# Last product of a down projection by quarters of the tokens: a hybrid encoder layer on one core

## The chip, the cores and the metric

The kernel runs on one NeuronCore of one Trainium2 chip. The metric is the device time of one execution in microseconds (us), median of the runs shown. Six names of engines occur: PE is TensorE's matrix multiplication, PEld its weight load, DVE is VectorE, ACT is ScalarE, POOL is GpSimd, and SP is SyncE, which here only issues DMA transfers. A letter q behind an engine (SPq, ACTq) means its queue of instructions.

## The reference, cut to what matters

One layer on 1024 tokens of width 1024: a normalised input, two attention mixers, an output projection with residual, then a gated MLP with residual, and a final RMS norm. The change lies in the last two lines:

```python
def rmsnorm(x, g):
    xf = x.astype(jnp.float32)
    y = xf * lax.rsqrt(jnp.mean(xf * xf, axis=-1, keepdims=True) + EPS)
    return (y * g.astype(jnp.float32)).astype(x.dtype)

def conv_gated_mlp(h, w_gate, w_up, conv_w, conv_b, w_down):
    ...
    return jnp.einsum('bsf,fd->bsd', jax.nn.silu(g) * u, w_down)

    h = h + conv_gated_mlp(hn, w_gate[l], w_up[l], conv_w[l], conv_b[l], w_down[l])
    return rmsnorm(h, norm_final)
```

The hidden width of the MLP is 2816, that is 22 tiles of 128, and `w_down` takes it back to 1024, that is 8 tiles of 128.

## The kernel before

Everything is held transposed: the 128 partitions carry 128 of the 1024 features, and the tokens run along the free dimension. `res[d]` (d from 0 to 7) is the residual stream of feature tile d, 128 partitions by 1024 tokens; the program's names in the profile show it as `h`. The tokens fall into two halves of 512 (`HALF`), h = 0 and h = 1, and `tsl(h)` is the slice of half h.

**Arithmetic.** Each fp32 operand is split into two fp32r parts, high and low, and a product of 128 hidden features takes three matmuls of 128 by 512: high by high, high by low, low by high. That is `group` (lines 797 to 799); every one of the three loads its own weights. Plain fp32 matmuls with a small moving operand (the sums `ss` and the spreadings `sw` below) show as two passes each in the trace.

**The down projection by seven products.** The product of w_down with the activations is cut into 2 by 2 blocks (features in lower and upper four tiles, hidden width in two halves of 11 tiles, tokens in two halves) and done as seven block products, `PRODUCTS`, p = 0 to 6. Within a product j runs over 0 to 3; a pair is the feature tiles j and j + 4. c runs over the three parts of the 11 hidden tiles (`PARTS`: 4, 4 and 3). `order` lists all (p, j, c), and from p = 1 on j is the outer of the two inner loops. Each step of the loop (line 1227 on) calls `prepare(i + 6, i + 4)`, which starts the loads of weights six steps ahead and splits the weights four steps ahead; then `group` for the step; then at most one task of `todo`. When a (p, j) is finished, `leave` is put in `todo`: DVE adds the PSUM bank to `res` (line 1188), and where that tile is then final, ACT squares it (line 1192) and DVE adds the square to a running sum (line 1197). Product 6 finishes tiles 4 to 7 of half 0; tiles 0 to 3 of half 0 and all tiles of half 1 are final before it. In the last `leave` (tile 7, half 0) the last square is not added; `inverse_narrow` takes both summands.

**The final norm.** `inverse_narrow` (line 145) sums the squares over the 128 partitions by matmuls with a column of ones, a token tile c of 128 at a time, into `ss`, column c; ACT takes the square root (line 153) and DVE the reciprocal (line 154). The result has the tokens on the partitions. `widen` (line 157) spreads it: a matmul per token tile of a broadcast column by the identity writes the factor of each token to all 128 partitions, into PSUM bank `sw` (line 161). [...] The tiles `y`, `wide`, `s2` and others share one tag (`tt`) with six buffers.

**The order of the end.** PE's order is the one written in the program (`manual_schedule` for PE); the other engines' orders are made by a scheduler from the program's order and its own estimates. Within product 6: after (j, c) = (0, 2) the `inverse_narrow` of half 1; after (1, 2) its `finish`; then pairs 2 and 3; and behind the last matmul, with nothing left for PE, the last `leave`, `inverse_narrow` and `finish` of half 0.

Of the kernel before, what the change touches and what calls it, by code (L numbers as in the profile page):

```python
# [15 lines left out]
AF = mybir.ActivationFunctionType  # L16
ALU = mybir.AluOpType
# [3 lines left out]
KT = D // 128  # L21
# [30 lines left out]
def hybrid_layer(tc, xT, w_in, w_out, w_gate, w_up, w_down, small, sink, rpb, consts, rope, out):  # L52
    nc = tc.nc
    with ExitStack() as ctx:
# [87 lines left out]
                acc = s2  # L142
            return acc

        def inverse_narrow(sqs, dim, tag):

            ps = bank("ss", tag)
            for c in range(4):
                for i, sq in enumerate(sqs):
                    nc.tensor.matmul(ps[:, c:c + 1], sq[:, c * 128:(c + 1) * 128], ones[:, 0:1], start=c == 0 and i == 0,  # L150
                                     stop=i == len(sqs) - 1, skip_group_check=True)
            v = cpool.tile([128, 4], F32, name="v4", tag="v4", bufs=4)
            nc.scalar.activation(v, ps[:, 0:4], AF.Sqrt, bias=eps, scale=float(D) / dim)
            nc.vector.reciprocal(v, v)
            return v

        def widen(v, tag):

            wide = bank("sw", tag)
            for c in range(4):  # L160
                nc.tensor.matmul(wide[:, c * 128:(c + 1) * 128], v[:, c:c + 1].to_broadcast([128, 128]), ident, start=True, stop=True)
            return wide

        def inverse_rms_wide(sq, dim, tag):
# [630 lines left out]
        def group(ps, ws, xs, first, last):  # L795
            for i, (w, x) in enumerate(zip(ws, xs, strict=True)):
                nc.tensor.matmul(ps, w[0], x[0], start=first and i == 0, stop=False, skip_group_check=True)  # L797
                nc.tensor.matmul(ps, w[0], x[1], start=False, stop=False, skip_group_check=True)  # L798
                nc.tensor.matmul(ps, w[1], x[0], start=False, stop=last and i == len(ws) - 1, skip_group_check=True)  # L799
# [384 lines left out]
            x_split(0, k)  # L1184
        sq, todo, vs = {}, [], {}

        def add(d, h, ps):
            nc.vector.tensor_tensor(res[d][:, tsl(h)], ps, res[d][:, tsl(h)], op=ALU.add)

        def square(d, h):  # L1190
            s2 = half("s2")
            nc.scalar.activation(s2, res[d][:, tsl(h)], AF.Square)
            if (d, h) == (KT - 1, 0):
                sq[h] = [sq[h], s2]
                return
            if h in sq:
                nc.vector.tensor_tensor(s2, s2, sq[h], op=ALU.add)
            sq[h] = s2

        def finish(h, v, tag):  # L1200
            wide = widen(v, tag)
            copy = half("wide")
            nc.scalar.activation(copy, wide, AF.Copy)
            for d in range(KT):
                y = half("y")
                x = res[d][:, tsl(h)]
                if d % 3 == 2:
                    nc.scalar.activation(y, x, AF.Copy, scale=col(C_NFIN + d))  # L1208
                    nc.gpsimd.tensor_tensor(y, y, copy, op=ALU.mult)  # L1209
                else:  # L1210
                    nc.vector.scalar_tensor_tensor(y, x, col(C_NFIN + d), wide, op0=ALU.mult, op1=ALU.mult)
                nc.sync.dma_start(out[d, :, tsl(h)], y)

        def leave(p, j, ps):

# [3 lines left out]
            else:  # L1219
                d, h = {1: (lo, 0), 2: (hi, 1), 3: (lo, 1), 4: (lo, 1), 5: (hi, 1), 6: (hi, 0)}[p]  # L1220
                add(d, h, ps)
                if p in (1, 4, 5, 6):
                    square(d, h)

        tags = lambda j, y: ("s", "s", "pt", "pt")[j] if y else ("pj", "pj", "o", "o")[j]
        banks = {}
        for i, (p, j, c) in enumerate(order):
            prepare(i + 6, i + 4)
            f, n = PARTS[c]
            if p in (0, 2, 3) and c == 0:  # L1230
                banks[p, j] = bank("dn", tags(j, p == 2))
            else:
                banks[p, j] = banks[{0: 0, 1: 0, 2: 2, 3: 3, 4: 2, 5: 3, 6: 3}[p], j]
            ps = banks[p, j]
            at_start, at_end = c == 0 and p in (0, 2, 3), c == 2
            group(ps, dws.pop((p, j, c)), [xs[p, f + q] for q in range(n)], at_start, at_end)
            if todo:
                todo.pop(0)()
            if at_end:
# [111 lines left out]
```

## Time and profile before

| | |
|---|---|
| median of 3 runs | 1128.92 us (1128.06 to 1130.89) |
| profiled execution | 1127.34 us |
| its span | 1125.6 us |
| granted TensorE clock, mean | 0.984 |

All times of rows below are from the start of that span. A row of the timeline gives the start, the duration, engine and line, the operation, output and inputs by name, the tile's shape, how many instructions the row merges, and in brackets how long the engine had been idle and what released it. A row of the windows view gives, for a stretch A:B, its length, then the busy time (and number of instructions) of PE, PEld, DVE, ACT and POOL, then the granted clock as a share of full speed, the busy share of the 16 DMA engines, and the GB/s moved. A matmul's duration holds its way through the pipeline; its cost in a stream is the distance to the next start.

### The profile page before, as it was taken

How to read it: one execution, taken by the hardware profiler on the slowest of the kernel's cores; microseconds unless marked ns; L12 is line 12 of the kernel's file. 1: busy time of each engine (PE TensorE's matmuls, PEld its weight loads, DVE VectorE, ACT ScalarE, POOL GpSimd, SP SyncE). 2: the span in 40 equal slices, each digit the busy share in tenths (PEclk: the TensorE clock that was granted, in tenths of full speed). 3: DMA queues.
4: the chain of work that ended last, by engine and by line, in shares of the span. 5: the costliest groups of instructions: out<-in, count | busy, mean ns of one | idle time of the engine just before them, and what ended most of it. 6: DMA issues, size and time to landing. Idle time of an engine off the chain costs nothing.

```text
span 1125.6 us, 14912 instructions
## 1 busy us (share of the span) xinstructions
PE 1086.2 (96%) x5124; PEld 903.0 (80%) x5124; DVE 852.4 (76%) x1549; ACT 548.3 (49%) x1033; POOL 105.7 (9%) x186
## 2 busy tenths in 40 slices
PE   8969999999999999999999999999999999999995
PEld 6858888888878877888788888888888878888884
DVE  6557888766689666989988778877877868797843
ACT  7235767655667433445434334334343645543531
POOL 0212332233223100000000000000000000000001
PEclk8989999999999999999999999999999999999997
DMA  7253220333215316412443223222322799875823
GB/s 266 65 122 80 53 57 29 84 92 87 75 31 148 103 47 211 163 47 78 166 160 122 105 92 123 102 103 94 122 103 94 244 302 294 268 221 174 272 83 144
DMA packets 67708, 147.03 MB, mean 131 GB/s; under 512 B 8112, under 2 KB 16816, under 8 KB 67632
## 3 DMA queue, kind: packets, MB, share of 16 engines
q1 hardware_dynamic: 57552, 121.04, 34.6%
q10 hardware_dynamic: 10080, 25.04, 5.9%
q8 instruction: 40, 0.66, 0.2%
q14 instruction: 36, 0.29, 0.1%
HBM read 103.58 MB, written 28.57 MB: 117 GB/s over the span
## 4 chain that ended last, share of the span: by engine, by line
PE 86%; DVE 7%; DMA 3%; ACT 2%; issue 2%; SPq 0%; POOLq 0%; ACTq 0%; DVEq 0%
PE pj L113 7%; PE pj L114 7%; PE pj L115 7%; PE dn L797 6%; PE dn L799 6%; PE dn L798 6%; PE z L799 5%; PE z L797 5%; PE z L798 5%; PE x L797 3%; PE x L799 3%; PE x L798 3%; PE s L273 3%; PE y L799 3%; PE y L797 3%; PE y L798 3%
## 5 line engine op out<-in xcount | busy, mean ns | idle before, releaser
L797 PE MATMUL dn<-xd,whi 128*128 128x512 f32 x308 | 120.2, 390 | 1.1 <-ACT c L1218 1.1
L786 ACT ACTIVATE whi<-ws 128x512 fp32r<-128x512 f32 (+1 forms) x100 | 60.1, 622 | 123.9 <-DVE ws L903 76.3
L799 PE MATMUL dn<-xd,wlo 128*128 128x512 f32 x308 | 119.8, 389 | 0.0
L798 PE MATMUL dn<-xd,whi 128*128 128x512 f32 x308 | 119.8, 389 | 0.0
L799 PE MATMUL z<-hg,wlo 128*128 128x512 f32 x264 | 103.1, 390 | 0.7 <-DVE wlo L787 0.7
L113 PE MATMUL pj<-xgh,whi 128*128 128x512 f32 x248 | 103.4, 417 | 0.0
L797 PE MATMUL z<-hg,whi 128*128 128x512 f32 x264 | 102.9, 390 | 0.0
L798 PE MATMUL z<-hg,whi 128*128 128x512 f32 x264 | 102.7, 389 | 0.0
L299 ACT ACTIVATE p<-p,nm 128x385 f32<-128x385 f32 (+3 forms) x128 | 75.1, 586 | 56.3 <-DVE nm L295 52.3
L115 PE MATMUL pj<-xgh,wlo 128*128 128x512 f32 x248 | 97.7, 394 | 0.0
L114 PE MATMUL pj<-xgl,whi 128*128 128x512 f32 x248 | 97.5, 393 | 0.0
L303 POOL TENSOR_SCALAR p<-p,sm 128x384 f32<-128x384 f32 (+1 forms) x128 | 73.5, 588 | 237.3 <-DVE sm L301 218.2
L787 DVE TENSOR_TENSOR wlo<-raw,whi 128x512 fp32r<-128x512 f32 (+1 forms) x102 | 66.3, 669 | 22.7 <-ACT whi L786 22.5
L787 DVE TENSOR_TENSOR wlo<-ws,whi 128x512 fp32r<-128x512 f32 (+1 forms) x100 | 66.7, 681 | 19.5 <-ACT whi L786 19.5
L309 DVE TENSOR_TENSOR pl<-pt,ph 128x384 fp32r<-128x384 f32 (+2 forms) x108 | 63.1, 588 | 23.2 <-ACT ph L308 22.1
L786 ACT ACTIVATE whi<-raw 128x512 fp32r<-128x512 f32 (+1 forms) x102 | 60.4, 611 | 41.4 <-DMA raw<-in_w_down_dram 18.4
L1108 ACT ACTIVATE xd<-xd 128x512 fp32r<-128x512 f32 x77 | 47.3, 627 | 58.0 <-DMA xd<-x 56.5
L308 ACT ACTIVATE ph<-pt 128x384 fp32r<-128x384 f32 (+2 forms) x108 | 55.3, 514 | 38.2 <-PE pt L408 30.8
L1209 POOL TENSOR_TENSOR y<-y,wide 128x512 f32<-128x512 f32 x4 | 5.1, 1283 | 727.0 <-ACT y L1208 727.0
L799 PE MATMUL y<-hg,wlo 128*128 128x512 f32 x176 | 68.7, 390 | 0.5 <-DVE wlo L787 0.5
L797 PE MATMUL x<-hg,whi 128*128 128x512 f32 x176 | 68.7, 390 | 0.0
L799 PE MATMUL x<-hg,wlo 128*128 128x512 f32 x176 | 68.5, 389 | 0.0
(199 smaller groups left out, 2657.8 us busy)
## 6 DMA issues: line engine op xcount, KB each, us to landing
xd<-x SPq DMA_DIRECT2D x77, 256.0 KB, 5.1
raw<-in_w_down_dram SPq DMA_DIRECT2D x72, 256.0 KB, 3.4
raw<-in_w_gate_dram SPq DMA_DIRECT2D x22, 512.0 KB, 3.5
raw<-in_w_up_dram SPq DMA_DIRECT2D x22, 512.0 KB, 4.0
x<-c ACTq DMA_DIRECT2D x22, 512.0 KB
raw<-in_w_in_dram SPq DMA_DIRECT2D x32, 256.0 KB, 3.2
raw<-in_w_down_dram SPq DMA_DIRECT2D x36, 192.0 KB, 3.8
x<-t ACTq DMA_DIRECT2D x11, 512.0 KB, 2.6
```

What stands on the lines that cost most here:

```text
L113: nc.tensor.matmul(ps, w[0], x[0][:, tsl(h)], start=first, stop=False)
L114: nc.tensor.matmul(ps, w[0], x[1][:, tsl(h)], start=False, stop=False)
L115: nc.tensor.matmul(ps, w[1], x[0][:, tsl(h)], start=False, stop=last)
L299: nc.scalar.activation(p[:, j, 0:e], p[:, j, 0:e], AF.Exp, bias=nm, scale=-1.0, accum_out=sm[:, j:j + 1])
L303: nc.gpsimd.tensor_scalar(p[:, i, 0:m], p[:, i, 0:m], sm[:, i:i + 1], 1.0, op0=ALU.mult, op1=ALU.mult)
L308: nc.scalar.activation(ph[:, 0:n], ps[:, 0:n], AF.Copy)
L309: nc.vector.tensor_tensor(pl[:, 0:n], ps[:, 0:n], f32(ph[:, 0:n]), op=ALU.subtract)
L786: nc.scalar.activation(hi, src, AF.Copy)
L787: nc.vector.tensor_tensor(lo, src, f32(hi[:, :, :]), op=ALU.subtract)
L797: nc.tensor.matmul(ps, w[0], x[0], start=first and i == 0, stop=False, skip_group_check=True)
L798: nc.tensor.matmul(ps, w[0], x[1], start=False, stop=False, skip_group_check=True)
L799: nc.tensor.matmul(ps, w[1], x[0], start=False, stop=last and i == len(ws) - 1, skip_group_check=True)
```

## The change

In product 6, pairs 2 and 3 are no longer done by 512 tokens but by 256: first both pairs for the first quarter of the tokens, then both for the second (the weights of both pairs are kept for that). Half 0's norm, outputs and stores are done for each quarter by itself: those of the first quarter between the matmuls of the second, those of the second behind the last matmul. `leave_quarter` adds and squares 256 columns. `widen` is called twice, into two banks, one read by DVE and one by ACT for the copy. Outputs overwrite `res` instead of going to `y`. The scaling of tiles 2 and 5 by the gain (`scaled`) is a call of its own, placed earlier, and these two tiles come last in `finish`. The second quarter's stores go alternately to SP's and ACT's queue. In `inverse_narrow` the loop over summands is now the outer one, everywhere.

```diff
-        def inverse_narrow(sqs, dim, tag):
+        def inverse_narrow(sqs, dim, tag, n=4):
 
             ps = bank("ss", tag)
-            for c in range(4):
-                for i, sq in enumerate(sqs):
+            for i, sq in enumerate(sqs):
+                for c in range(n):
                     nc.tensor.matmul(ps[:, c:c + 1], sq[:, c * 128:(c + 1) * 128], ones[:, 0:1], start=c == 0 and i == 0,
                                      stop=i == len(sqs) - 1, skip_group_check=True)
...
-        def widen(v, tag):
+        def widen(v, tag, n=4):
 
             wide = bank("sw", tag)
-            for c in range(4):
-                nc.tensor.matmul(wide[:, c * 128:(c + 1) * 128], v[:, c:c + 1].to_broadcast([128, 128]), ident, start=True, stop=True)
+            for c in range(n):
+                nc.tensor.matmul(wide[:, c * 128:(c + 1) * 128], v[:, c:c + 1].to_broadcast([128, 128]), ident,
+                                 start=c == 0, stop=True, skip_group_check=True)
...
-            if (d, h) == (KT - 1, 0):
-                sq[h] = [sq[h], s2]
-                return
...
-        def finish(h, v, tag):
-            wide = widen(v, tag)
+        APART = (2, 5)
+
+        def scaled(d, h):
+            x = res[d][:, tsl(h)]
+            nc.scalar.activation(x, x, AF.Copy, scale=col(C_NFIN + d))
+
+        def finish(h, v, cols=whole, split=False):
+            n = (cols.stop - cols.start) // 128
+            wide, again = widen(v, "pt", n), widen(v, "pt", n)
             copy = half("wide")
-            nc.scalar.activation(copy, wide, AF.Copy)
-            for d in range(KT):
-                y = half("y")
-                x = res[d][:, tsl(h)]
-                if d % 3 == 2:
-                    nc.scalar.activation(y, x, AF.Copy, scale=col(C_NFIN + d))
-                    nc.gpsimd.tensor_tensor(y, y, copy, op=ALU.mult)
+            nc.scalar.activation(copy[:, cols], again[:, 0:128 * n], AF.Copy)
+            for i, d in enumerate([d for d in range(KT) if d not in APART] + list(APART)):
+                x = at_res(d, h, cols)
+                if d in APART:
+                    nc.gpsimd.tensor_tensor(x, x, copy[:, cols], op=ALU.mult)
                 else:
-                    nc.vector.scalar_tensor_tensor(y, x, col(C_NFIN + d), wide, op0=ALU.mult, op1=ALU.mult)
-                nc.sync.dma_start(out[d, :, tsl(h)], y)
+                    nc.vector.scalar_tensor_tensor(x, x, col(C_NFIN + d), wide[:, 0:128 * n], op0=ALU.mult, op1=ALU.mult)
+                (nc.scalar if split and i % 2 else nc.sync).dma_start(out[d, :, h * HALF + cols.start:h * HALF + cols.stop], x)
...
+        def leave_quarter(j, ps, cols):
+
+            x = at_res(j + NP, 0, cols)
+            add(j + NP, 0, ps, cols)
+            s2 = parts[cols.start, j] = half("s2")[:, cols]
+            nc.scalar.activation(s2, x, AF.Square)
+            if j + NP < KT - 1:
+                nc.vector.tensor_tensor(s2, s2, sq[0][:, cols], op=ALU.add)
...
-            group(ps, dws.pop((p, j, c)), [xs[p, f + q] for q in range(n)], at_start, at_end)
+            if p < 6 or j < 2:
+                group(ps, dws.pop((p, j, c)), [xs[p, f + q] for q in range(n)], at_start, at_end)
...
             if p == 6 and (j, c) == (0, 2):
+                for d in APART:
+                    scaled(d, 1)
                 vs[1] = inverse_narrow([sq[1]], D, "s")
             if p == 6 and (j, c) == (1, 2):
-                finish(1, vs[1], "pt")
-        for t in todo:
-            t()
-        finish(0, inverse_narrow(sq[0], D, "s"), "pt")
+                finish(1, vs[1])
+
+
+        parts = {}
+        for k, cols in enumerate(quarters):
+            for j in (2, 3):
+                ps = banks[6, j]
+                for c, (f, n) in enumerate(PARTS):
+                    group(ps[:, cols], dws[6, j, c], [[y[:, cols] for y in xs[6, f + q]] for q in range(n)], False, c == 2)
+                    if todo:
+                        todo.pop(0)()
+                    if (k, j, c) == (0, 3, 0):
+                        for d in APART:
+                            scaled(d, 0)
+                    if (k, j, c) == (1, 2, 0):
+                        vs[0] = inverse_narrow([parts[0, 2], parts[0, 3]], D, "s", 2)
+                    if (k, j, c) == (1, 2, 1):
+                        finish(0, vs[0], quarters[0])
+                leave_quarter(j, ps, cols)
+        first = quarters[1].start
+        finish(0, inverse_narrow([parts[first, 2], parts[first, 3]], D, "s", 2), quarters[1], True)
```

Two things of the changed program's order of instructions are not in the diff. The scheduler moves three of the four `scaled` operations further forward on ACT, to just behind the squares of their tiles (tile 2 of half 0 as far as product 1); the one of tile 5, half 0, stands behind its last square in product 6. And in the last `finish` it puts POOL's stores forward: SP issues those of tiles 0, 2, 3, 6 in this order, ACT those of tiles 1, 5, 4, 7, though tiles 2 and 5 are POOL's and come last in the program. The stores of the first quarter keep the program's order on SP.

More of the change, by code (lines that the diff above doesn't have):

```diff
@@ L152, in inverse_narrow @@
             v = cpool.tile([128, 4], F32, name="v4", tag="v4", bufs=4)
-            nc.scalar.activation(v, ps[:, 0:4], AF.Sqrt, bias=eps, scale=float(D) / dim)
-            nc.vector.reciprocal(v, v)
+            nc.scalar.activation(v[:, 0:n], ps[:, 0:n], AF.Sqrt, bias=eps, scale=float(D) / dim)
+            nc.vector.reciprocal(v[:, 0:n], v[:, 0:n])
             return v
-        def widen(v, tag):
+        def widen(v, tag, n=4):
             wide = bank("sw", tag)
-            for c in range(4):
-                nc.tensor.matmul(wide[:, c * 128:(c + 1) * 128], v[:, c:c + 1].to_broadcast([128, 128]), ident, start=True, stop=True)
+            for c in range(n):
+                nc.tensor.matmul(wide[:, c * 128:(c + 1) * 128], v[:, c:c + 1].to_broadcast([128, 128]), ident,
+                                 start=c == 0, stop=True, skip_group_check=True)
             return wide
@@ L1185, in hybrid_layer, with add @@
         sq, todo, vs = {}, [], {}
-        def add(d, h, ps):
-            nc.vector.tensor_tensor(res[d][:, tsl(h)], ps, res[d][:, tsl(h)], op=ALU.add)
+        whole, quarters = slice(0, HALF), (slice(0, HALF // 2), slice(HALF // 2, HALF))
+        at_res = lambda d, h, cols: res[d][:, h * HALF + cols.start:h * HALF + cols.stop]
+        def add(d, h, ps, cols=whole):
+            x = at_res(d, h, cols)
+            nc.vector.tensor_tensor(x, ps[:, cols], x, op=ALU.add)
         def square(d, h):
@@ L1198, in square @@
             sq[h] = s2
[L1200 to L1212 removed]
+        APART = (2, 5)
[5 more added lines that the diff above has]
+            wide, again = widen(v, "pt", n), widen(v, "pt", n)
+            copy = half("wide")
+            nc.scalar.activation(copy[:, cols], again[:, 0:128 * n], AF.Copy)
+            for i, d in enumerate([d for d in range(KT) if d not in APART] + list(APART)):
+                x = at_res(d, h, cols)
+                if d in APART:
+                    nc.gpsimd.tensor_tensor(x, x, copy[:, cols], op=ALU.mult)
+                else:
+                    nc.vector.scalar_tensor_tensor(x, x, col(C_NFIN + d), wide[:, 0:128 * n], op0=ALU.mult, op1=ALU.mult)
+                (nc.scalar if split and i % 2 else nc.sync).dma_start(out[d, :, h * HALF + cols.start:h * HALF + cols.stop], x)
         def leave(p, j, ps):
@@ L1235, in hybrid_layer @@
             at_start, at_end = c == 0 and p in (0, 2, 3), c == 2
-            group(ps, dws.pop((p, j, c)), [xs[p, f + q] for q in range(n)], at_start, at_end)
+            if p < 6 or j < 2:
+                group(ps, dws.pop((p, j, c)), [xs[p, f + q] for q in range(n)], at_start, at_end)
             if todo:
                 todo.pop(0)()
-            if at_end:
+            if at_end and (p < 6 or j < 2):
                 todo.append(lambda p=p, j=j, ps=ps: leave(p, j, ps))
```

## The prediction

> **What bounds the kernel now.** I read the page first, then the timeline of the last 33 us, then the same end by windows.
>
> ```profile
> span 1125.6 us, 14912 instructions
> ...
> PE 1086.2 (96%) x5124; PEld 903.0 (80%) x5124; DVE 852.4 (76%) x1549; ACT 548.3 (49%) x1033; POOL 105.7 (9%) x186
> ...
> PE 86%; DVE 7%; DMA 3%; ACT 2%; issue 2%; SPq 0%; POOLq 0%; ACTq 0%; DVEq 0%
> ```
>
> PE sets the time nearly everywhere, so more work put among its matmuls is paid in full. The exception is the end:
>
> ```profile
> 1093.68 1.05 PE L161 MATMUL sw<-cst,v 128*128 128x128 f32 x8
> ...
> 1094.49 0.48 PE L797 MATMUL dn<-xd,whi 128*128 128x512 f32 x1
> ...
> 1094.81 0.39 PE L798 MATMUL dn<-xd,whi 128*128 128x512 f32 x1
> ...
> 1109.34 0.39 PE L799 MATMUL dn<-xd,wlo 128*128 128x512 f32 x1
> ...
> 1109.77 0.69 DVE L1188 TENSOR_TENSOR h<-dn,h 128x512 f32<-128x512 f32 x1 [5.29 <-PE dn L799]
> 1110.50 0.63 ACT L1192 ACTIVATE s<-h 128x512 f32<-128x512 f32 x1 [6.74 <-DVE h L1188]
> 1111.18 1.72 PE L150 MATMUL ss<-ones,s 128*128 128x1 f32 x14 [1.33 <-ACT s L1192]
> 1112.94 0.26 ACT L153 ACTIVATE v<-ss,eps 128x4 f32<-128x4 f32 x1 [1.81 <-PE ss L150]
> 1113.23 0.18 DVE L154 RECIPROCAL v<-v 128x4 f32<-128x4 f32 x1 [2.77 <-ACT v L153]
> 1113.47 2.08 PE L161 MATMUL sw<-cst,v 128*128 128x128 f32 x8 [0.57 <-DVE v L154]
> 1115.63 0.60 ACT L1203 ACTIVATE wide<-sw 128x512 f32<-128x512 f32 x1 [2.43 <-PE sw L161]
> ...
> 1116.26 2.72 DVE L1211 SCALAR_TENSOR_TENSOR y<-h,par,sw 128x512 f32<-128x512 f32 x4 [2.85 <-ACT wide L1203]
> 1116.91 1.27 POOL L1209 TENSOR_TENSOR y<-y,wide 128x512 f32<-128x512 f32 x1 [15.80 <-ACT y L1208]
> 1117.04 5.54 SPq L1212 DMA_DIRECT2D out_dram<-y  x8
> ...
> 1121.29 0.75 DVE L1211 SCALAR_TENSOR_TENSOR y<-h,par,sw 128x512 f32<-128x512 f32 x1 [0.67 <-POOL y L1209]
> ```
>
> From 1094.81 to 1109.34 the matmuls start 14.53 / 64 = 0.227 us apart, so the last slot ends at 1109.57. From there to the end, 16.03 us, a chain runs in which each engine waits for the one before: add, square, sums, root, reciprocal, spreading, outputs, stores. The change shortens this chain and pays with work in PE's stream.
>
> **What the stream pays.** (a) The spreading of half 1 is done twice. Eight passes take 1094.49 - 1093.68 = 0.81 us, so +0.81. (b) 66 matmuls of 512 columns become 132 of 256, each with its own weight load. Now 66 x 0.227 = 14.98 us. The 256-column price is in the attention stage:
>
> ```profile
> 223.93 0.28 PE L419 MATMUL o<-ph,v 128*128 128x256 f32 x1
> ...
> 224.40 0.40 PE L113 MATMUL pj<-xgh,whi 128*128 128x512 f32 x1
> 231.80 0.19 PEld L420 LDWEIGHTS o<-pl,v 128*128 128x128 f32 x1
> 231.91 0.19 PEld L113 LDWEIGHTS pj<-xgh,whi 128*128 128x128 f32 x1
> 1085.25 0.95 PE L150 MATMUL ss<-ones,s 128*128 128x1 f32 x8
> 1086.06 0.49 PE L797 MATMUL dn<-xd,whi 128*128 128x512 f32 x1
> ```
>
> Between the first two rows stand four 256-column matmuls: 0.47 / 4 = 0.1175 us each. A run of 132 has no long matmul in between to load weights behind; but loads that follow each other closely, among 128-column matmuls, start 0.11 us apart (the two PEld rows), just under 0.1175. I take 0.1175: 15.51 us, +0.53. Bounds: 0.1135, half of 0.227, gives 0; 0.188, a load's whole shown duration of 0.19, gives +9.8 and is a rival. (c) The first quarter's sums and spreadings stand among the matmuls, four matmuls of two passes each. The sums of half 1 cost 1086.06 - 1085.25 = 0.81, and the first 512-column matmul behind such a block takes 0.32 (1094.49 to 1094.81) instead of 0.227, so 0.90 each, +1.80. Together +3.14: the last slot now ends at 1109.57 + 3.14 = 1112.71.
>
> PE should meet no new wait. The first matmul of the second quarter, which starts at 1093.68 + 1.62 + 0.09 + 7.76 = 1103.15, waits for DVE's add of tile 6's first quarter. Ahead of that on DVE stand six multiplies of half 1 from about 1094.8 (5 x 0.66 + 0.75, to 1098.9) and one add of squares (to about 1099.6); its own data come at 1095.39 + 33 x 0.1175 = 1099.27, so it is done near 1100, 3 us early. The first quarter's sums stand 12 matmuls (1.41 us) behind its last matmul, and add and square need about 0.2 + 0.42 + 0.04 + 0.41 = 1.07; its spreading again 12 matmuls behind the sums, root and reciprocal needing 0.6. If that cover failed, PE would wait for the few tenths that lack. The `scaled` operations moved forward, 0.7 us each, go into an ACT that is busy 49%, between weight splits that run four steps ahead (12 x 0.227 = 2.7 us a step): nothing; without that cover at most three of them, 2.1 us. The `y` buffers that went back to stores cost nothing on PE before and nothing now. The first quarter's stores start near 1107.9 and are over near 1113, before the last ones. The reordered sums elsewhere keep their number: nothing.
>
> **What the chain saves.** Shorter operations come from groups of lines by shape, the stores from windows.
>
> ```profile
> L309 DVE TENSOR_TENSOR pl<-pt,ph 128x256 fp32r<-128x256 f32 x16 | 6.7, 420 | 7.0 <-ACT ph L308 6.9
> L786 ACT ACTIVATE whi<-raw 128x384 fp32r<-128x384 f32 x12 | 6.2, 517 | 7.6 <-DMA raw<-in_w_down_dram 6.2 <-PE dn L798 1.4
> L308 ACT ACTIVATE ph<-pt 128x256 fp32r<-128x256 f32 x16 | 6.1, 381 | 11.9 <-PE pt L408 11.8
> L303 POOL TENSOR_SCALAR p<-p,sm 128x384 f32<-128x384 f32 x96 | 58.7, 623 | 154.4 <-DVE sm L301 138.7 <-PE pt L408 15.7
> L303 POOL TENSOR_SCALAR p<-p,sm 128x256 f32<-128x256 f32 x32 | 15.3, 483 | 82.9 <-DVE sm L301 79.5 <-PE pt L408 3.4
> L373 POOL TENSOR_TENSOR xb<-cst,rr 128x256 f32<-128x256 f32 x8 | 9.1, 1143 | 0.0
> L1212 SPq DMA_DIRECT2D out_dram<-y x16: 332/338/454, 1096.2 to 1122.2; - x16
> 10.00:11.00 1.00, 0.00 (x0) 0.00 (x0) 0.00 (x0) 1.00 (x1) 0.00 (x0) 0.86 1.04 422
> 70.00:70.50 0.50, 0.05 (x1) 0.00 (x0) 0.50 (x3) 0.07 (x1) 0.00 (x0) 1.00 0.24 60
> 72.00:72.50 0.50, 0.00 (x0) 0.00 (x0) 0.00 (x0) 0.50 (x3) 0.00 (x0) 0.66 0.02 0
> 1113.20:1113.30 0.10, 0.00 (x0) 0.00 (x0) 0.07 (x1) 0.00 (x1) 0.00 (x0) 0.61 0.00 0
> 1117.50:1118.00 0.50, 0.00 (x0) 0.00 (x0) 0.50 (x2) 0.00 (x0) 0.50 (x1) 0.50 0.24 90
> 1118.00:1118.50 0.50, 0.00 (x0) 0.00 (x0) 0.50 (x2) 0.00 (x0) 0.18 (x1) 0.50 1.05 389
> 1124.00:1124.50 0.50, 0.00 (x0) 0.00 (x0) 0.00 (x0) 0.00 (x0) 0.00 (x0) 0.50 0.36 135
> ```
>
> Add: 0.69 becomes 0.42, -0.27. Square: 0.63 for 512, 0.517 for 384, so 0.41 for 256, -0.22. Sums: 14 passes in 1.72 are 0.113 apart plus 0.25 for the last; behind the last square only 4 are left, 3 x 0.113 + 0.25 = 0.59, -1.13. Root and reciprocal stay.
>
> Spreading: from 1113.47 to DVE's first output at 1116.26 it was 2.79, since DVE also waited for ACT's copy. Now DVE reads its own bank after two matmuls, four passes. At full clock (1.05 for eight) they take 0.64, at half clock (2.08 for eight) 1.22; with a gap of 0.08 that is -2.07 or -1.49. The granted clock fell to half inside 1113.20 to 1113.30, 3.65 us after the last slot; earlier, after a stream that ended at 70.05, inside 72.00 to 72.50, at about 72.16, 2.1 us after. The new spreading stands 2.28 to 2.92 us after the last slot, between these two: I take full clock at 6 in 10. [...]
>
> Outputs and stores: before, 1116.26 to 1125.6, 9.34 us. After, counted from DVE's first output: DVE takes 0.48 and then 0.39 each (512 columns: 0.75 and 0.66; 0.27 less), the sixth ends at 2.43. POOL waits for the second spreading (+0.40) and the copy (0.38 and gaps), starts at 0.82. A POOL multiply by 256: 0.64, half of 1.27, or 1.14 (L373) are the ends; L303's slope leaves 0.20 fixed, so 0.20 + 1.07 / 2 = 0.74. POOL ends at 1.56 and 2.30. Because POOL's stores stand forward in both queues, ACT's stores of tiles 4 and 7 wait behind tile 5's: at 0.34 an issue the last starts near 3.0 instead of 2.46. Data flow 0.84 after the issue (first issue at 1117.04; the 0.12 us worth of bytes in 1117.50 to 1118.00 puts the start at 1117.88). The rate with the stores' rows of 2 KB is 389 GB/s, and 422 where loads with rows of 4 KB run; over 16 engines a row takes 84 and 155 ns, so an estimated 49 ns for the new rows of 1 KB, 0.39 us a store. Ends: 0.34 (same rate) and 0.68 (same time a row). At 0.39 the data of the last four follow each other from 3.2 to 4.8. The end came 1.4 after the last data (1124.18, by the 135 GB/s of the last window): 6.2 us, -3.1 (0.34: -3.4; 0.68: -1.4).
>
> Sum: -0.27 - 0.22 - 1.13 - 2.07 - 3.1 = -6.8 on the chain, +3.14 on the stream: -3.65 us, a span of 1121.95. The profiled execution took 1127.34, 1.6 under the median of 1128.92; taking the change off the median gives 1125.3.
>
> The second queue buys little: eight issues at 0.34 on SP alone would end near 3.3 instead of 3.0. [...] My sum has one stream of data for both; two at once would end at 3.0 + 0.84 + 0.39 = 4.2 instead of 4.8, 0.6 us sooner.
>
> **Rivals.** (1) The tail goes slower than I sum: half clock, POOL and small rows. Half clock alone delays DVE by 0.58 and POOL's path by 1.04, and the last store hangs on POOL: gain 2.6, time 1126.3. Rows at 0.68 alone: gain 2.0, 1126.9; POOL at 1.14 adds up to 0.8. For it: the clock fell after 2.1 us once, and all three prices are from neighbours. Against: each needs its bad end. Typical gain 2.2: 1126.7. (2) Weight loads don't keep up in a run of 132: at 0.188 a matmul the stream pays 9.8 instead of 0.53, a net loss of 5.6: 1134.5. It turns the sign from 0.145 a matmul on. For it: no run longer than four is in the trace. Against: 0.11 between loads. (3) The change doesn't do what it says: the first quarter's outputs still crowd the end, because DVE's multiplies for it (from 1107.5 to 1110.0) delay the second quarter's adds. By the sum DVE is through with them and with tile 6 at 1111.2, 1.7 before tile 7 needs it, so they would have to run 4.7 us longer to take 3 us from the gain: gain 0.6, 1128.3.
>
> **How the numbers follow.** Forecast 0.55 (gain 3.0 to 4.6, with the bounds of (b) and of the store), rival 1 0.31, rival 2 0.07, rival 3 0.07. About 0.3% (3.4 us) is what a measurement can tell here, as the three runs spread over 0.25%; so the forecast lies at that bound, and part of its cases falls within it. Faster 0.49: nearly nine tenths of the forecast's; same 0.43: the rest of it, rivals 1 and 3; slower 0.08. The range from 1123.8 (gain 5.1, runs' spread included) to 1128.2 takes in rival 1 and most of rival 3.
>
> **What would show it.** In the profile after: 256-column matmuls 0.117 apart (rival 2: 0.14 and more); no idle PE before the last slot, at about 1112.7; the last spreading at full clock, or not; DVE's outputs 0.39 apart and POOL's near 0.74; the last store issued near 6.0 us after the last slot, and the end 9.2 after it. Wrong would be a PE wait within the two quarters, or a chain of more than 10.5 us.

## The result, and the profile after

| | before | changed |
|---|---|---|
| median | 1129.17 us of 18 runs (1126.52 to 1133.97) | 1126.01 us of 18 runs (1121.92 to 1129.26) |
| ratio to before, 95% interval | | 0.9968 (0.9956 to 0.9980) |
| span of the profiled execution | 1125.6 us | 1121.3 us |

The ratio is worth -3.6 us (-5.0 to -2.3); the sum had said -3.65. The change is faster by about 0.3%, an amount close to what can be told from nothing.

The spans differ by 4.3 us, but not all of that is the change's. I read every profile here from one mark, the start of half 1's spreading, to the end of the span. What lies ahead of that mark differs from profile to profile: it stood at 1092.54 in one profile of a kernel and at 1099.30 in another of the same kernel. Behind the mark the two kernels that were profiled twice agree within 0.06 us (28.81 and 28.77, 27.06 and 27.00, each time with the last spreading at full clock). So measured, it was 31.92 us before (1093.68 to 1125.6) and is 28.81 after: the change earns 3.1 us there, and the other 1.2 us lie ahead of it.

The page of the changed kernel, its first part (PE was busy for 1086.2 us before, with 82 instructions less):

```profile
span 1121.3 us, 15082 instructions
...
PE 1085.5 (97%) x5206; PEld 906.3 (81%) x5206; DVE 853.1 (76%) x1559; ACT 548.4 (49%) x1037; POOL 105.8 (9%) x188
```

The timeline of its end (start, duration, engine, line, operation; the matmuls left out follow each other without a gap):

```profile
1092.49 1.95 PE L161 MATMUL sw<-cst,v 128*128 128x128 f32 x16
1094.19 0.36 PE L798 MATMUL dn<-xd,whi 128*128 128x256 f32 x1
1094.40 0.28 PE L799 MATMUL dn<-xd,whi 128*128 128x256 f32 x1
...
1103.63 0.95 PE L150 MATMUL ss<-ones,s 128*128 128x1 f32 x8
1104.44 0.36 PE L798 MATMUL dn<-xd,whi 128*128 128x256 f32 x1
...
1111.88 0.50 PE L150 MATMUL ss<-ones,s 128*128 128x1 f32 x4
1112.08 0.42 DVE L1193 TENSOR_TENSOR h<-dn,h 128x256 f32<-128x256 f32 x1 [1.74 <-PE dn L800]
1112.54 0.42 ACT L1238 ACTIVATE s<-h 128x256 f32<-128x256 f32 x1 [2.65 <-DVE h L1193]
1113.01 0.61 PE L150 MATMUL ss<-ones,s 128*128 128x1 f32 x4 [0.62 <-ACT s L1238]
1113.65 0.26 ACT L153 ACTIVATE v<-ss,eps 128x2 f32<-128x2 f32 x1 [0.69 <-PE ss L150]
1113.94 0.17 DVE L154 RECIPROCAL v<-v 128x2 f32<-128x2 f32 x1 [1.44 <-ACT v L153]
1114.26 1.13 PE L161 MATMUL sw<-cst,v 128*128 128x128 f32 x8 [0.65 <-DVE v L154]
1114.98 2.44 DVE L1219 SCALAR_TENSOR_TENSOR h<-h,par,sw 128x256 f32<-128x256 f32 x6 [0.87 <-PE sw L161]
1115.42 0.38 ACT L1213 ACTIVATE wide<-sw 128x256 f32<-128x256 f32 x1 [1.51 <-PE sw L161]
1115.88 1.42 POOL L1217 TENSOR_TENSOR h<-h,wide 128x256 f32<-128x256 f32 x2 [6.94 <-ACT wide L1213]
```

In the kernel before, `finish` makes a half's eight output tiles, six on DVE from the bank of the spreading and tiles 2 and 5 on ACT (the gain) and POOL (from `wide`, ACT's copy of that bank), with a store behind each. In the rows above DVE's six are L1219, POOL's two L1217.

The reader is to see two lengths: the stream, from the mark to 1111.88, where the last matmul slot ends, 19.39 us (before 15.89); and the chain from there to 1121.3, 9.42 us (before 16.03). The chain is the same one, with nearly every link shorter (root and reciprocal stay) and the last spreading at full clock.

Groups of lines by shape, and windows of the end (busy times, granted clock, share of the DMA engines, GB/s):

```profile
L798 PE MATMUL dn<-xd,whi 128*128 128x256 f32 x44 | 12.7, 288 | 0.0
L1217 POOL TENSOR_TENSOR h<-h,wide 128x256 f32<-128x256 f32 x4 | 2.8, 734 | 16.7 <-ACT wide L1213 16.7
L1220 ACTq DMA_DIRECT2D out_dram<-h x4: 345/385/406, 1115.9 to 1118.3; - x4
```

```profile
1118.00:1119.00 1.00, 0.00 (x0) 0.00 (x0) 0.00 (x0) 0.00 (x0) 0.00 (x0) 0.50 1.03 336
1119.00:1120.00 1.00, 0.00 (x0) 0.00 (x0) 0.00 (x0) 0.00 (x0) 0.00 (x0) 0.50 0.96 314
```

PE waits for nothing in the two quarters (0.0 idle before these 44 matmuls, and before the 44 of each of the two other lines). The last store is issued at 1118.3, 6.4 us behind the last slot, and the data flow at 336 GB/s until about 1119.93 (314 GB/s over 1 us is 0.93 us at that rate).

### The profile page after: what moved, and what is told of

It is laid out like the page before. It is cut to its first block, busy times and chain, and to the rows that moved or that the text cites. A ratio compares the mean times of both kernels' runs of the same rounds, so it can differ in the third digit from the quotient of the medians.

```text
span 1121.3 us, 15082 instructions
## 1 busy us (share of the span) xinstructions
PE 1085.5 (97%) x5206; PEld 906.3 (81%) x5206; DVE 853.1 (76%) x1559; ACT 548.4 (49%) x1037; POOL 105.8 (9%) x188
## 4 chain that ended last, share of the span: by engine, by line
PE 86%; DVE 7%; DMA 2%; ACT 2%; issue 2%; SPq 0%; DVEq 0%; ACTq 0%
PE pj L113 7%; PE pj L114 7%; PE pj L115 7%; PE dn L798 6%; PE dn L799 6%; PE dn L800 6%; PE z L800 5%; PE z L798 5%; PE z L799 5%; PE x L798 3%; PE x L799 3%; PE s L274 3%; PE x L800 3%; PE y L800 3%; PE y L799 3%; PE y L798 3%
## 5 line engine op out<-in xcount | busy, mean ns | idle before, releaser
L798 PE MATMUL dn<-xd,whi 128*128 128x512 f32 (+1 forms) x330 | 124.2, 376 | 2.8 <-ACT c L1226 2.8
L800 PE MATMUL dn<-xd,wlo 128*128 128x512 f32 (+1 forms) x330 | 123.7, 375 | 0.0
L799 PE MATMUL dn<-xd,whi 128*128 128x512 f32 (+1 forms) x330 | 123.7, 375 | 0.0
L1217 POOL TENSOR_TENSOR h<-h,wide 128x256 f32<-128x256 f32 (+1 forms) x6 | 5.4, 921 | 724.5 <-ACT wide L1213 724.5
L798 PEld LDWEIGHTS dn<-xd,whi 128*128 128x128 f32 x330 | 62.1, 188 | 14.4 <-ACT c L1226 3.2
L799 PEld LDWEIGHTS dn<-xd,whi 128*128 128x128 f32 x330 | 62.1, 188 | 11.1
L800 PEld LDWEIGHTS dn<-xd,wlo 128*128 128x128 f32 x330 | 62.1, 188 | 11.1
```

## The experiments

Every kernel's three marks, from its timeline and its page:

| kernel | mark | last slot | end | stream | chain | sum | ratio, 95% interval |
|---|---|---|---|---|---|---|---|
| before | 1093.68 | 1109.57 | 1125.6 | 15.89 | 16.03 | 31.92 | 1 |
| changed | 1092.49 | 1111.88 | 1121.3 | 19.39 | 9.42 | 28.81 | 0.9968 (0.9956 to 0.9980) |
| changed, again | 1093.13 | 1112.51 | 1121.9 | 19.38 | 9.39 | 28.77 | 0.9965 (0.9945 to 0.9986) |
| quarters in the matmuls only | 1097.91 | 1114.64 | 1130.6 | 16.73 | 15.96 | 32.69 | 1.0024 (1.0004 to 1.0043) |
| changed, no quarters | 1098.04 | 1114.82 | 1128.5 | 16.78 | 13.68 | 30.46 | 1.0005 (0.9988 to 1.0021) |
| changed, one queue | 1095.84 | 1115.22 | 1124.9 | 19.38 | 9.68 | 29.06 | 0.9965 (0.9948 to 0.9983) |
| changed, outputs in `y` | 1093.14 | 1112.53 | 1125.9 | 19.39 | 13.37 | 32.76 | 1.0006 (0.9986 to 1.0026) |
| changed, cut at 384 | 1096.63 | 1121.49 | 1128.9 | 24.86 | 7.41 | 32.27 | 1.0009 (0.9992 to 1.0026) |
| one bank early | 1095.62 | 1113.67 | 1124.0 | 18.05 | 10.33 | 28.38 | 0.9966 (0.9950 to 0.9983) |
| the same, POOL one tile | 1092.54 | 1110.58 | 1119.6 | 18.04 | 9.02 | 27.06 | 0.9973 (0.9955 to 0.9992) |
| the same, again | 1099.30 | 1117.35 | 1126.3 | 18.05 | 8.95 | 27.00 | 0.9956 (0.9934 to 0.9978) |
| the same, one bank last | 1095.99 | 1114.04 | 1123.5 | 18.05 | 9.46 | 27.51 | not timed |
| before, matmuls added | 1096.46 | 1112.35 | 1128.0 | 15.89 | 15.65 | 31.54 | not timed |

My theory was the sum of the prediction. The rivals that the experiments address are: that the price of the stream is set by weight loads and lies elsewhere than I read it; that most of the gain comes from another part than the quarters; and that the clock, not the shorter chain, decides.

**The matmuls by quarters alone.** The kernel before, with pairs 2 and 3 of product 6 by 256 tokens and nothing else changed:

```diff
-            group(ps, dws.pop((p, j, c)), ...)
+            if p < 6 or j < 2:
+                group(ps, dws.pop((p, j, c)), ...)
...
+        for k in range(2):
+            cols = slice(k * HALF // 2, (k + 1) * HALF // 2)
+            for j in (2, 3):
...
+                    group(ps[:, cols], dws[6, j, c], ..., False, c == 2)
...
+                if k == 1:
+                    todo.append(lambda j=j, ps=ps: leave(6, j, ps))
```

> The kernel before, with only the matmuls of pairs 2 and 3 of product 6 by 256 tokens; norm, outputs and stores of half 0 as a whole behind the last one. The stretch from the start of half 1's spreading to the end was 31.9 us before and 28.8 after. My theory (quarters cost PE a little in the stream; what they earn, they earn by the shorter chain): 132 matmuls 0.120 us apart take 15.8 instead of 15.0, the chain keeps its 16 us, stretch 32.8, ratio to before 1.0008. Rival (256 columns cost nothing): 15.0, stretch 31.9, ratio 1.0000. Rival (loads fall behind): 0.188 apart, stretch above 41, ratio 1.009.

The stream grew by 0.84 us (16.73 against 15.89) and the chain stayed (15.96). That is the price of the cut, paid for nothing: the ratio too is above 1. Of the expectations, both rivals are out (nothing, and loads that fall behind). In the changed kernel 77 matmuls stand between 1094.40 and 1103.63: 0.120 us each, where I had taken 0.1175.

**All but the quarters.** The changed kernel with the half as one piece:

```diff
-        whole, quarters = slice(0, HALF), (slice(0, HALF // 2), slice(HALF // 2, HALF))
+        whole, quarters = slice(0, HALF), (slice(0, HALF),)
...
-        first = quarters[1].start
-        finish(0, inverse_narrow([parts[first, 2], parts[first, 3]], D, "s", 2), quarters[1], True)
+        finish(0, inverse_narrow([parts[0, 2], parts[0, 3]], D, "s"), whole, True)
```

> The changed kernel without the quarters: outputs in place, two banks, the early scaling, two queues, but half 0 as one piece behind the last matmul. My theory (about half of the gain is the quarters'): the stream pays 0.9 for the doubled spreading of half 1; the chain saves 0.7 in the sums, 0.7 by the two banks (1.7 with the clock full) and 1.2 in outputs and stores: stretch 30.2 (29.8 to 31.5 by the clock at the last spreading), ratio 0.9985. Rival (the gain is that of the outputs in place, the banks and the queues; quarters only move it): stretch 28.8, ratio 0.997.

Its timeline:

```profile
1116.43 1.05 PE L150 MATMUL ss<-ones,s 128*128 128x1 f32 x8 [0.66 <-ACT s L1238]
1118.14 2.02 PE L161 MATMUL sw<-cst,v 128*128 128x128 f32 x16 [0.66 <-DVE v L154]
1119.31 4.04 DVE L1219 SCALAR_TENSOR_TENSOR h<-h,par,sw 128x512 f32<-128x512 f32 x6 [1.31 <-PE sw L161]
```

The mark to the end is 30.46 us. The other parts earn 1.46 us here (31.92 to 30.46): fewer sums behind the last square (1.05 against 1.72), and DVE's first output 1.17 us behind the start of the spreading instead of 2.79, part of it because this spreading ran at full clock. The quarters earn 1.65 more: they cost 2.6 in the stream and take 4.3 off the chain. This split rests on one profile of each kernel: in whole times the kernel without quarters gains nothing that can be told (ratio 1.0005, 0.9988 to 1.0021), so the 1.46 us are seen behind the mark alone.

**Outputs in `y` again.** The changed kernel with new tiles for the outputs:

```diff
+                y = half("y")[:, cols]
...
-                    nc.gpsimd.tensor_tensor(x, x, copy[:, cols], op=ALU.mult)
+                    nc.gpsimd.tensor_tensor(y, x, copy[:, cols], op=ALU.mult)
...
```

> The changed kernel with the outputs in tiles y of the shared six buffers, as before, instead of in place. Theory (in place is one of the parts that earn what the quarters alone do not): the last quarter's eight outputs need buffers that the squares, the copy and the first quarter's stores still hold, so DVE and POOL wait for slots: 1 to 2 us in the tail, stretch 30 to 31, with waits of DVE on a store's DMA in the chain. Rival: the first quarter's stores are over about 5 us before the last outputs, so slots are free and only the last two outputs wait: stretch 28.8 to 29.3.

Its chain that ended last, in order of time, and its timeline at the same place:

```profile
1110.07 3.16 DMA out_dram<-y
...
1113.57 0.73 POOL y L1218
...
1115.25 1.88 PE ss L150 x8
```

```profile
1114.32 0.42 ACT L1239 ACTIVATE s<-h 128x256 f32<-128x256 f32 x1 [6.24 <-POOL y L1218]
1115.25 1.86 PE L150 MATMUL ss<-ones,s 128*128 128x1 f32 x8 [2.56 <-DVE s L1241]
1117.76 2.05 PE L161 MATMUL sw<-cst,v 128*128 128x128 f32 x8 [0.64 <-DVE v L154]
```

Mechanism right, size wrong, twice over: 32.76 instead of the expected 30 to 31. The last quarter's outputs do wait for stores, but the costly wait is earlier. A store of the first quarter holds a buffer; POOL's output needs it; ACT's square of tile 6 stands behind POOL's output; DVE's addition behind the square; and the sums, all eight passes of them, behind the addition. PE waits 2.56 us with its stream already at its end, and the spreading then falls into half clock. Part of the 3.95 us between this kernel and the changed one is not the buffers' own: the store that POOL's output waits for, issued at 1110.07, took 1.81 us to issue, against 0.33 to 0.40 for the four before it. The changed kernel has such an issue too (1.90 us at 1109.49), and nothing waits for it there. What makes an issue so long was not tried. Without outputs in place the quarters lose 0.84 us against the kernel before.

**One queue for the last stores.** The changed kernel, `split` left out in the last `finish`.

> The changed kernel with the last quarter's stores all on SP. My theory (both queues share the data path; a second one saves issue time only, at most 0.4 us, and SP in the program's order no longer waits for POOL in the middle): stretch 28.8 to 29.2, ratio 0.997. Rival (the stall seen on SP in the first quarter, where the sixth of eight stores took 1.9 us to issue, belongs to eight close stores of 128 KB on one queue): one issue of about 1.9 us again, stretch 30.3, ratio 0.998.

Windows of its end, and its stores by line:

```profile
1120.00:1121.00 1.00, 0.00 (x0) 0.00 (x0) 0.76 (x2) 0.00 (x0) 0.64 (x1) 0.68 0.82 269
1121.00:1122.00 1.00, 0.00 (x0) 0.00 (x0) 0.00 (x0) 0.00 (x0) 0.00 (x0) 0.50 0.80 263
...
L1220 SPq DMA_DIRECT2D out_dram<-h x8: 332/396/405, 1118.8 to 1122.2; - x8
```

The second queue is worth 0.26 us (29.06 against 28.81, the chain 9.68 against 9.42). Eight issues from 1118.8 to 1122.2 are 0.49 apart, and 131 KB in 0.49 us are the 263 and 269 GB/s that flow: one queue is bound by its issues, where two move 336. The rival's long issue is not among these eight, the longest of which took 0.405 us.

**The cut at 384.** Pieces of 384 and 128 columns (`quarters` as `slice(0, 384), slice(384, HALF)`, three and one token tiles in the sums).

> The changed kernel with the half cut at 384 and 128 columns instead of 256 and 256. Theory (a weight load in front of each matmul sets a floor of about 0.11 us, just under the 0.120 us seen for 256 columns): 384-column matmuls 0.175 apart, 128-column ones 0.11 apart and not 0.06; the 66 + 66 matmuls take 66 x 0.285 = 18.8 instead of 15.8, +3.0 on the stream; the first piece's spreading has 12 passes instead of 8 (+0.4) and six sums instead of four (+0.2 or so), the last piece's chain gets shorter by about 1.5 to 2 us (fewer passes, shorter outputs; stores bound by issue at 0.45 us each as before). Stretch from half 1's spreading to the end: 30.3 to 31. Rival: no floor, the price is per column (0.06 for 128 columns): the stream stays at 15.8 and the stretch falls to 27.5.

Its timeline, and its windows:

```profile
1098.94 0.34 PE L798 MATMUL dn<-xd,whi 128*128 128x384 f32 x1
...
1101.54 0.33 PE L798 MATMUL dn<-xd,whi 128*128 128x384 f32 x1
...
1113.85 2.87 PE L161 MATMUL sw<-cst,v 128*128 128x128 f32 x12
...
1119.14 0.27 PE L798 MATMUL dn<-xd,whi 128*128 128x128 f32 x1
...
1121.15 0.28 PE L798 MATMUL dn<-xd,whi 128*128 128x128 f32 x1
```

```profile
1110.38:1113.79 3.41, 3.41 (x33) 3.41 (x33) 0.41 (x2) 0.79 (x2) 0.00 (x0) 1.00 0.00 0
1113.75:1113.80 0.05, 0.05 (x3) 0.05 (x2) 0.00 (x0) 0.00 (x0) 0.00 (x0) 0.89 0.00 0
1113.85:1117.15 3.30, 3.30 (x18) 3.30 (x17) 1.67 (x4) 0.39 (x1) 0.00 (x0) 0.50 0.06 21
1117.20:1117.25 0.05, 0.05 (x3) 0.05 (x2) 0.05 (x1) 0.05 (x1) 0.00 (x0) 0.98 1.37 461
```

There is a floor for matmuls that each load their own weights: 384 columns cost 2.60 / 15 = 0.173 us, 128 columns 2.01 / 18 = 0.112, and not a quarter of the 0.227 of 512 columns. Between 256 columns (0.120) and 128 a narrower matmul buys next to nothing. That the weight load is what sets the floor is argued from the 0.11 us between loads in the prediction's rows; matmuls without a load were not tried. The sum is 32.27 where 30.3 to 31 was expected, because the clock fell to half in the middle of the stream, from 1113.79 to 1117.20, on a PE that the windows show busy all the time. Twelve passes took 2.52 us there until the next matmul (at 0.107, 1.28), six matmuls 1.1 us instead of 0.70 behind the sums: 1.6 us, and without it an estimated 30.7. The chain did get shorter, by 2.0 us, and the stream longer by 5.5, or 3.9 without the half clock.

**One bank where PE is the bound.** The changed kernel with the second bank only in the last quarter:

```diff
-            wide, again = widen(v, "pt", n), widen(v, "pt", n)
+            wide = widen(v, "pt", n)
+            again = widen(v, "pt", n) if split else wide
```

> The changed kernel with one spreading into one bank for half 1 and for the first quarter; only the last quarter keeps two. My theory: these two spreadings stand in a PE stream that sets the time, so each pass taken away is paid in full: eight passes of half 1 less, 0.85 us (the 16 passes took 1.70), and four of the first quarter, 0.42 us. From the start of half 1's spreading to the end of the span 28.8 - 1.27 = 27.5 us; ratio to the kernel before about 0.9957. Rival A: the second bank was worth its price because DVE and ACT share a bank badly: DVE's multiplies of half 1 then start later (by the copy, about 0.6 us) and hold up the add that the second quarter's first matmul waits for; PE shows a wait there and the stretch stays at 28.8. Rival B: the extra passes fill time that PE would lose otherwise (the first matmul behind the block waits for its weights): the stretch falls by less than 0.6, to above 28.2.

Its timeline, and windows around the fall of its clock:

```profile
1116.05 2.04 PE L161 MATMUL sw<-cst,v 128*128 128x128 f32 x8 [0.64 <-DVE v L154]
1117.28 2.44 DVE L1220 SCALAR_TENSOR_TENSOR h<-h,par,sw 128x256 f32<-128x256 f32 x6 [1.38 <-PE sw L161]
1118.59 1.41 POOL L1218 TENSOR_TENSOR h<-h,wide 128x256 f32<-128x256 f32 x2 [7.86 <-ACT wide L1214]
```

```profile
1112.45:1113.67 1.22, 1.22 (x12) 1.22 (x11) 0.43 (x1) 0.09 (x1) 0.00 (x0) 1.00 0.84 280
1115.80:1115.85 0.05, 0.00 (x0) 0.00 (x0) 0.05 (x1) 0.00 (x0) 0.00 (x0) 1.00 0.00 0
1115.85:1115.90 0.05, 0.00 (x0) 0.00 (x0) 0.05 (x1) 0.00 (x0) 0.00 (x0) 0.56 0.00 0
```

The stream fell by 1.34 us, as the theory of passes paid in full had it (1.27); rival B, under 0.6, is out. The sum fell by only 0.43, since this execution met the half clock: the clock fell 2.2 us behind the last slot, the spreading took 2.04 us, DVE started 0.51 later and POOL 0.92 later than in the changed kernel, and the end came 0.91 later. It is the half clock of the prediction's first rival, seen in a run.

**POOL with one tile.** The same, with tile 5 on DVE in the last quarter, and the scaling of tile 5 by the gain on ACT kept to the first quarter; and again beside the changed kernel.

```diff
-            for i, d in enumerate([d for d in range(KT) if d not in APART] + list(APART)):
+            apart = APART[:1] if split else APART
+            for i, d in enumerate([d for d in range(KT) if d not in apart] + list(apart)):
...
-                        for d in APART:
-                            scaled(d, 0)
+                        for d, cols5 in ((2, whole), (5, quarters[0])):
+                            x5 = at_res(d, 0, cols5)
+                            nc.scalar.activation(x5, x5, AF.Copy, scale=col(C_NFIN + d))
```

> As the kernel with one bank early, and in the last quarter POOL makes only tile 2 while DVE makes tile 5 too (seven outputs), so that no store on ACT's queue waits behind POOL's second output. Theory (the end is set by the last issue: tile 7 was ready 0.84 us before its store was issued, behind tile 5's): the last issue moves from 6.4 us behind the last slot to about 6.0, and the end with it by 0.3 to 0.4: stretch about 27.1, ratio about 0.9953. Rival A: the end is set by the stream of data (341 GB/s, 0.38 us a store): the last data end where they did, stretch 27.5. Rival B: DVE's seventh output (0.39 us) becomes the last link: stretch 27.5 to 27.9.

> The kernel with one bank early and POOL with one tile once more, beside the changed kernel as it is. Theory: 1.75 us less from half 1's spreading to the end, so a ratio to the kernel before about 0.0015 under the changed kernel's (0.9953 if that is 0.9968), whatever the time of the part before the spreading does. At half clock in the last spreading 0.5 of it is lost. Rival: the ratio doesn't differ by as much, since the time ahead of the spreading varies by more than this from run to run.

> The changed kernel as it is, for comparison on the same chip: ratio to the kernel before 0.9968, and 28.8 us from half 1's spreading to the end where the last spreading runs at full clock, 29.7 at half clock (the price of half clock at POOL's start was 0.92).

The chain is 9.02 and 8.95 instead of 9.42, the sum 27.06 and 27.00: 1.75 us under the changed kernel, as expected. Its windows:

```profile
1116.00:1117.00 1.00, 0.00 (x0) 0.00 (x0) 0.51 (x2) 0.00 (x0) 0.00 (x0) 0.50 1.02 343
1117.00:1118.00 1.00, 0.00 (x0) 0.00 (x0) 0.00 (x0) 0.00 (x0) 0.00 (x0) 0.50 0.99 340
```

The data now flow without a pause at 340 GB/s, so I read the end as hanging on the first output and on 1 MB of stores, no more on the last issue. In whole times it cannot be told from the changed kernel, as the rival had it: the ratios are 0.9973 and 0.9956 against 0.9968 and 0.9965, each with an interval of about 0.002 to either side. The part ahead of the mark, 1092.54 and 1099.30 in two profiles of it, varies by far more than 1.75 us.

**One bank in the last quarter too.** The kernel with POOL's one tile, with `again = wide` everywhere:

> The kernel with one bank early and POOL with one tile, with the last quarter's factors in one bank too (four passes, DVE and ACT read the same bank). Theory (two banks earn their four passes in the last quarter only, because there DVE's first output need not stand behind ACT's copy): DVE's first output comes 3.5 us behind the last slot instead of 3.1, as in the first quarter, where one bank put 1.06 us between the start of the spreading and DVE's first output and two banks 0.64; POOL starts 0.4 earlier; the stores flow from the first output on, so the end moves by +0.4: 9.4 behind the last slot instead of 9.0. Rival: POOL's tile or the last issue sets the end: 9.0 or below.

```profile
1116.41 0.83 PE L161 MATMUL sw<-cst,v 128*128 128x128 f32 x4 [0.64 <-DVE v L154]
1117.70 2.83 DVE L1221 SCALAR_TENSOR_TENSOR h<-h,par,sw 128x256 f32<-128x256 f32 x7 [1.43 <-ACT wide L1214]
```

The chain is 9.46 (expected 9.4): DVE stands behind ACT's copy, and its first output comes 3.66 us behind the last slot instead of 3.10. Some 0.15 of that is the clock, which fell during the spreading (four passes took 0.83, against 0.68 in the cut at 384). So in these profiles, one of each form, the second bank is worth about 0.3 us here, and in the two earlier places it only cost.

**Matmuls to hold the clock.** The kernel before with seven more matmuls of 512 columns behind its last one, into a bank that nothing reads:

> The kernel before, with seven more 512-column matmuls into an unused bank right behind the last product (1.6 us, while DVE and ACT add and square). My theory (the last spreading took 2.08 us for its eight passes because the granted clock had fallen to half 3.65 us after the stream): clock 1.00 through the spreading, 1.05 us for the eight, stretch 30.9. Rival (the long passes are those of a PE that starts from rest, whatever the clock): 2.08 stays, stretch 31.9.

```profile
1112.35 1.75 PE L1258 MATMUL fill<-xd,whi 128*128 128x512 f32 x7
...
1113.93 1.84 PE L150 MATMUL ss<-ones,s 128*128 128x1 f32 x16
...
1116.34 1.67 PE L161 MATMUL sw<-cst,v 128*128 128x128 f32 x8 [0.57 <-DVE v L154]
```

Half a result: the spreading took 1.67 us instead of 2.08, its first passes at full clock and the rest at half, and the sum fell by 0.4. The rival, a PE that is slow because it starts from rest, is out: this spreading came after 0.57 us of rest too, and its passes were slow only from the fall of the clock, at 1116.81, on. PE was busy until 1115.77, from 1113.93 on with sums of one column; why the clock fell all the same was not shown.

## Why the prediction was right, point by point

**The stream.** Forecast +3.14, measured +3.50. The doubled spreading cost 0.89 instead of 0.81: its block takes 1.70 (1092.49 to 1094.19). The two blocks of the first quarter are right: 1103.63 to 1104.44 is 0.81, and the first slot behind a block of passes is 0.21 (1094.19 to 1094.40) instead of 0.120, so 0.90 each. The mis-sized term is the 256-column matmul: 132 x 0.120 is 15.84, +0.86 instead of +0.53. I read 0.1175 from four matmuls among wider ones; a run of 132 costs 0.0025 more each. Rival 2 was right that there is a floor, and it may be the weight load's, but it lies at 0.11, just under 0.120, and decides nothing at 256 columns.

**No wait on PE.** Right, but not for the reason that I gave most room. DVE was early, as said. Rival 3 is out: when the data of the last tile came, DVE had been idle for 1.74 us (row at 1112.08). The cover that mattered is the one that I passed over in half a sentence: the outputs in place. I said that the `y` buffers had cost PE nothing before, which holds; that the quarters would turn them into a wait of PE behind the last slot, 2.56 us of the 3.95 that outputs in `y` cost, and that outputs in place are what keeps it away, I did not see. There the forecast was lucky.

**The chain.** Forecast 9.24 us behind the last slot, measured 9.42. Add, square, sums, root, spreading and the first output came 3.10 behind it (3.00 by the forecast's terms). DVE's six outputs took 2.44 us (2.43), POOL's 0.734 each (0.74), and the data ran at 336 GB/s, which is the 0.39 us a store worked out from the two row sizes. The last issue came 3.28 behind the first output instead of 3.0: issues stood 0.44 to 0.49 apart, not 0.34. Tile 7 was ready at 1117.42 and issued at 1118.3, behind tile 5's store, as the order had said.

**The second queue.** Forecast 0.3, measured 0.26, right by two errors that cancel: one queue issues more slowly than I took, and the last store of two queues is later too. Issue time was the bound of the one queue (265 against 336 GB/s). A second stream of data is not seen: from 1117.5 to 1119.5 of the changed kernel the packets of the two queues took 58.8% and 37.7% of the 16 DMA engines' time, 96.5% together.

**The clock.** The last spreading ran at full clock, which I gave 6 in 10. In the seven profiles whose last quarter has the changed kernel's form the clock fell, in the order of the table, 4.3, 5.3, 5.1, 2.2, 5.1, 3.9 and 2.8 us behind the last slot; the spreading starts 2.4 behind it. One of the seven met half clock from its first pass, and one in its last pass. That makes 6 in 10 look low, though seven profiles cannot decide it; the price of rival 1, 1.04 at POOL, was 0.92. The clock also weighs in the 3.1 us behind the mark: before, the last spreading ran at half clock and took 2.08 us, 1.03 more than the 1.05 of half 1's, and in the changed kernel it ran at full clock. So about 1 us of the 3.1 hangs on the clock that the two executions met. What makes the clock fall was not shown: in the profile with 2.2, PE had run the last product's matmuls up to 2.2 us before the fall (busy 1.22 of 1.22 us from 1112.45 to 1113.67).

**The size.** -3.65 forecast; -3.1 behind the mark in the profiles, -3.6 by the ratio with an interval that holds both. The sum over-stated the gain by 0.36 in the stream and 0.18 in the chain. That the ratio meets the sum almost exactly is luck.

**Still open.** Why the part ahead of the mark varies by up to 6.8 us between profiles was not tried. The traces give a lead: the longer the clock stood at half between the first time that it was full and the mark, the later the mark. It was 17.1 us in the profiles with 1092.49 and 1092.54, and 30.7 us in the one with 1099.30; over the thirteen profiles I estimate about half a microsecond for each of them (a straight line, correlation 0.85). That the shorter version beats the changed kernel is shown only behind the mark, not in whole times.

## What to carry to other kernels

Cut the last product so that only a small piece of the norm, the outputs and the stores is left behind the last matmul, and pay for it in the stream with the price of a long run of the narrower matmul, not of a few among wider ones; near the floor of such matmuls (0.112 us at 128 columns here) a narrower cut cost more in the stream than it took off the chain (5.5 us, or 3.9 without the half clock, against 2.0). Before cutting, look for shared buffers that the earlier piece's stores still hold: here such a wait reached back through POOL, ACT and DVE to PE's sums (2.56 us). Spend extra passes, such as a second copy of a factor, only where PE has nothing else to do: behind the last matmul the second bank was worth about 0.3 us, among the matmuls it cost 1.34.

## What the runs showed of the hardware

The distances between two falls of the granted clock went in steps of 3.413 us here. In seven profiles rows of 0.05 us hold both the fall near 72 us and the last one. Between the two lie 1041.065 us (before, and the cut at 384), 1044.478 (the changed kernel, both profiles), 1047.892 (one queue, and POOL's one tile again) and 1051.305 (no quarters): each distance is 3.413 or 3.414 us from the next. In the cut at 384 the half clock lasted as long, 3.413 us (1113.789 to 1117.202). For the changed kernel, in windows of 0.05 us (the fall lies inside the row with 0.76, and inside that with 0.54):

```profile
71.70:71.75 0.05, 0.00 (x0) 0.00 (x0) 0.00 (x0) 0.05 (x3) 0.00 (x0) 0.76 0.00 0
...
1116.20:1116.25 0.05, 0.00 (x0) 0.00 (x0) 0.05 (x2) 0.00 (x0) 0.05 (x1) 0.54 0.00 0
```

That is 71.726 and 1116.204. Where the last fall stands to the last slot differs between two profiles of one program: it came 4.3 and 5.3 us behind it, and 5.1 and 3.9. In these four it came behind the last spreading, so no pair here shows one program with its last spreading once at full and once at half clock.

A busy PE did not keep the clock up in the cut at 384: from 1110.38 to 1113.79 PE was busy 3.41 of 3.41 us, with matmuls of 128 columns and twelve sums of one column, and the clock fell at the end of that stretch. What the clock goes by stays open.
